# Latent attention: three heads' probabilities divided on ScalarE, turned in squares on VectorE and placed by transfers

## The chip, the core and the metric

The kernel runs on one core of a Trainium2 chip. The core has a matrix engine, TensorE (PE in the profile; PEld is its weight load), a vector engine (VectorE, DVE), a scalar engine (ScalarE, ACT), a general engine (GpSimd, POOL) and a sync engine (SyncE, SP) that here only issues transfers (DMAs). Each engine works through its own instructions in the order in which they were written; semaphores make one wait for another. Operands lie in SBUF (128 partitions), matrix products land in PSUM, of which this kernel uses seven banks in turn for products, and everything else is in the chip's main memory. The metric is the device time of one launch in microseconds (us).

## What is computed

Two layers (DEPTH = 2) over 256 tokens of width 1024, all in float32. The first layer's token mixer is latent attention with 8 heads, the second's is forgetting attention with 8 heads. Around each mixer stand two SwiGLU feed-forward blocks, and behind each layer a gated embedding is added. The change is in latent attention, whose core is this:

```python
def causal_block_attention(scores_fn, v, chunk_causal):
    for q0 in range(0, seq, Q_BLOCK):           # two blocks of 128 queries
        q1 = q0 + Q_BLOCK                       # block reads keys [0, q1)
        s = scores_fn(q0, q1)
        s = jnp.where(allowed, s, NEG_INF)
        probs = jax.nn.softmax(s, axis=-1).astype(v.dtype)
        outs.append(jnp.einsum('bhqk,bkhd->bqhd', probs, v[:, :q1]))

def mla_mixer(u, cos, sin, w_down, q_norm, w_uq, kv_norm, w_ukv, w_o):
    ...
    def scores(q0, q1):
        sc = (jnp.einsum('bqhd,bkhd->bhqk', q_nope[:, q0:q1], k_nope[:, :q1])
              + jnp.einsum('bqhr,bkr->bhqk', q_rope[:, q0:q1], k_rope[:, :q1]))
        return sc.astype(jnp.float32) * scale
    o = causal_block_attention(scores, v, chunk_causal=True)
    return o.reshape(b, s, MLA_HEADS * MLA_V) @ w_o
```

A head has three 128 x 128 blocks of probabilities: queries 0 to 127 against keys 0 to 127, and queries 128 to 255 against both key halves. The kernel holds them side by side, queries on the partitions, as one 128 x 384 tile. To multiply them with the values, TensorE needs keys on the partitions, so each head's 128 x 384 tile has to be turned.

## The kernel before

**Products.** Large products are computed as high times high, high times low and low times high, where a float32 operand is split into a rounded high half and the remainder as its low half. ScalarE writes the high half (L97 for weights, L559 for the heads' outputs), VectorE the low half (L101, L228). Weights come in pieces of 128 x 1024 through four raw buffers and seven pairs of high and low; a new fetch is issued on SP when VectorE has made a low half and so freed a raw buffer.

**Attention.** The function `attention` serves both mixers; `lag` is 3 for latent attention (called `late` in the code) and 2 for forgetting attention. It runs one loop of `H + lag` steps, and step h works on several heads at once. In latent attention step h does, in this order: `shares(h-2)`, the division of the probabilities by their sums (VectorE, L520 to L522); `low`, the low half of the output of the head whose values came last (VectorE, L228); `project(h)`, some remaining projections of queries and values; `turn(h-3)`, three transposes on TensorE (L543) and their evacuation by ScalarE into the tile ptS (L545); `scores(h-1)` (TensorE L782 and L784; maximum on VectorE L501, negated and scaled L505; exponentials with their sums on ScalarE L513 and L514); some units of the output projection (`fill_some`, L247 and L248); and `values(h-3)`, two products each for the two key halves (TensorE L557 and L558) with the evacuation of the high half by ScalarE (L559).

**Fills.** The output projection needs all heads, but a unit (one 128-column block of the output, one head) can run as soon as that head's high and low halves are there. A table `MLA_FILLS` gives the number of units for each step, and `ready` is the number of heads whose output the units may read. Up to four output blocks are open at once, each holding one PSUM bank. They fill TensorE while it would otherwise have too little to do.

**Forgetting attention.** Its first six heads (`moved=H - 2`) are already turned in another way: VectorE transposes the 32 x 32 squares inside the 128 x 384 tile (L526), four transfers put the squares in their places in main memory (L531) and one transfer reads the tile back (L536). The values product then reads the tile in the squares' order.

**Order of work.** There is no scheduler: the order on each engine is the order in which the code writes the instructions. Buffers rotate: 4 of the tile pr (probabilities), 3 of ptS (turned probabilities), 2 in main memory.

Of the kernel before, what the change touches and what calls it, by code (L numbers as in the profile page):

```python
# [11 lines left out]
F32 = mybir.dt.float32  # L12
# [7 lines left out]
P = 128  # L20
# [5 lines left out]
H = 8  # L26
# [114 lines left out]
def trunk(ctx, tc, xT, xt, pT, pos, freq, bf, lead0, lead1, ffn_in, ffn_out, w_down, w_uq, w_ukv, mla_o,  # L141
# [85 lines left out]
    def rest(hi, lo, src):  # L227
        nc.vector.tensor_sub(lo, src, hi.bitcast(F32))  # L228
# [255 lines left out]
            pass  # L484


    def attention(project, score, v, mask, scale, nxt, lag, fills, early, cumq=None, moved=0, room=None):
        late = lag > 2
        os = act.tile([P, H, 2, T], F32R, name="os", tag="u")
        probs = {}  # L490
        turned = {}
        lows = []

        def scores(h):
            ps = bank("psc", (P, 3 * P))
            score(h, (ps[:, :P], ps[:, P:]))
            m = work.tile([P, 2], F32, name="m", bufs=3)
            pr = work.tile([P, 3 * P], F32, name="pr", bufs=4)

            for i, a in enumerate((slice(0, P), slice(P, 3 * P))):  # L500
                nc.vector.tensor_tensor_reduce(pr[:, a], ps[:, a], mask(h)[i], 1.0, NEG, op0=ALU.add,  # L501
                                               op1=ALU.max, accum_out=m[:, i:i + 1])
            nm = work.tile([P, 2], F32, name="nm", bufs=3)
            if cumq is None:
                nc.vector.scalar_tensor_tensor(nm, m, -1.0, scale, op0=ALU.mult, op1=ALU.mult)  # L505
# [7 lines left out]
            nc.scalar.activation(pr[:, :P], pr[:, :P], AF.Exp, bias=nm[:, 0:1], scale=by[0], accum_out=den[:, 0:1])  # L513
            nc.scalar.activation(pr[:, P:], pr[:, P:], AF.Exp, bias=nm[:, 1:2], scale=by[1], accum_out=den[:, 1:2])  # L514
            probs[h] = pr, den

        def shares(h):
            pr, den = probs[h]
            inv = work.tile([P, 2], F32, name="inv", bufs=3)
            nc.vector.reciprocal(inv, den)  # L520
            nc.vector.tensor_scalar(pr[:, :P], pr[:, :P], inv[:, 0:1], None, op0=ALU.mult)
            nc.vector.tensor_scalar(pr[:, P:], pr[:, P:], inv[:, 1:2], None, op0=ALU.mult)  # L522
            if h < moved:
                pr, _ = probs.pop(h)
                squares = room[h % 2]
                nc.vector.transpose(squares.rearrange("p (k u c) -> p k u c", k=4, u=3),  # L526
                                    pr.rearrange("p (u k c) -> p k u c", u=3, k=4))
                turned[h] = dram.tile([P, 3 * P], F32, name="keys", bufs=2)
                to = turned[h].rearrange("(k r) (q n) -> q r k n", k=4, q=4)
                for q in range(4):  # L530
                    nc.sync.dma_start(to[q], squares[q * 32:(q + 1) * 32, :].rearrange("r (k n) -> r k n", k=4))  # L531

        def back(h):

            p = work.tile([P, 3 * P], F32, name="ptS", bufs=3)
            nc.sync.dma_start(p, turned[h])  # L536
            turned[h] = p

        def turn(h):
            pr, _ = probs.pop(h)  # L540
            pt = bank("pt", (P, 3 * P))
            for i in range(3):
                nc.tensor.transpose(pt[:, i * P:(i + 1) * P], pr[:, i * P:(i + 1) * P], ident)  # L543
            turned[h] = work.tile([P, 3 * P], F32, name="ptS", bufs=3)
            nc.scalar.activation(turned[h], pt, AF.Copy)  # L545

        def values(h):
            p = turned.pop(h)
            po = bank("po", (P, T))
            if h < moved:  # L550
# [6 lines left out]
            nc.tensor.matmul(to[0], v[:, 0, h * P:(h + 1) * P], p[0], start=True, stop=False)  # L557
            nc.tensor.matmul(to[1], v[:, 1, h * P:(h + 1) * P], p[1], start=False, stop=True)  # L558
            nc.scalar.activation(os[:, h, 0, :], po, AF.Copy)  # L559
            lows.append((os[:, h, 0, :], os[:, h, 1, :], po))  # L560

        def low():

            while lows:
                rest(*lows.pop())


        ws, pss, upto = {}, {}, {}
        ready = 0

        def fill(d, n):
            if d not in ws:
                ws[d], = W.get()

                pss[d] = bank("ps2", (P, 2, T) if d < KD - 3 else (P, T))
            if upto.setdefault(d, 0) < n:
                part(pss[d], ws[d], os, range(upto[d], n), H - 1)
                upto[d] = n

        def fill_some(n):  # L580
            while n > 0:
                d = min(ws, key=lambda d: (upto[d], d), default=None)
                if d is None or upto[d] >= ready:
                    if len(ws) == early:
                        return
                    d = len(ws)
                    upto[d] = 0
                m = min(ready - upto[d], n)
                if m <= 0:
                    return  # L590
                fill(d, upto[d] + m)
                n -= m

        def finish(d):
            W.done(ws[d])
            src = hT[:, d, :]
            for p in parts(pss[d]):
                nc.vector.tensor_add(src, p, src)
# [12 lines left out]

        for h in range(H + lag):
            if 0 <= h - 2 < H:
                shares(h - 2)
            low()
            if h == H and not late:
                W.pump()
            if late:

                ready = h - lag - 1  # L620
            if h < H:
                project(h, 0)
            fill_some(fills.get((h, 0), 0))
            if 0 <= h - lag < moved:
# [37 lines left out]
    def mla(norm, nxt):  # L662
# [26 lines left out]

        kq, v, kr = keys_values()  # L690
        kT, qT, qr = kq[:, :8, :], kq[:, 8:16, :], kq[:, 16:24, :]
        held = []
        halves = slice(0, ROPE), slice(ROPE, P)

# [89 lines left out]
                nc.tensor.matmul(dst[t], qr[:, h, t * P:(t + 1) * P], kr[:, h % 2, :(t + 1) * P], start=False,  # L784
                                 stop=t == 1)

        attention(project, score, v, lambda h: (chunks[:, P:], chunks), qscale, nxt, 3, MLA_FILLS, 4)


    def fox(norm, nxt):  # L790
# [98 lines left out]
        attention(project, score, v, lambda h: (early[:, h, :], drops[:, h, :]), FOX_SCALE, nxt, 2, FOX_FILLS, 4, cumq=cumq, moved=H - 2, room=squares)  # L889


    class Embedding:
# [429 lines left out]
```

## Time and profile before

| | before |
|---|---|
| median of 3 runs | 986.46 us (985.97 to 987.25) |
| profiled execution, its own time | 986.36 us |
| its span, first to last instruction | 984.5 us |
| TensorE busy | 975.1 us, 99% of the span |
| VectorE, ScalarE, GpSimd busy | 75%, 52%, 44% |
| granted TensorE clock, mean | 0.999 |
| latent attention's loop over heads | about 214 to 246 us of the span |
| VectorE busy from 215 to 240 us | 21.21 of 25 us |
| ScalarE busy from 215 to 240 us | 18.38 of 25 us |

The profile comes from one execution, and all positions are microseconds from the start of its span. In a timeline row stand the start, the duration, the engine, the line of the code, the operation, the tile written and the tile read, the shape and how many instructions were merged; in square brackets the time that the engine sat idle before and what ended it. Neighbouring instructions of one engine overlap, so what an instruction costs its engine is the distance of two starts rather than its duration.

### The profile page before, as it was taken

The numbers are of one execution on the slowest core, as the hardware profiler recorded it, in microseconds if no ns is written. First come the engines' busy times: TensorE is split into PE (matmuls) and PEld (weight loads), VectorE is DVE, ScalarE is ACT, GpSimd is POOL, SyncE is SP. The second block draws the span as 40 slices with busy tenths as digits, with TensorE's granted clock in tenths as the row PEclk, the third lists the DMA queues.
The fourth block names the chain that finished last, engine by engine and source line by source line (L and its number), as shares of the span: only waits on it lengthen the run. The fifth ranks groups of instructions, "written<-read, shape, count | busy, mean of one in ns | idle before, by whom it ended". The sixth has DMA issues, their size and how long they took to land.

```text
span 984.5 us, 15920 instructions
## 1 busy us (share of the span) xinstructions
PE 975.1 (99%) x5762; PEld 861.6 (88%) x5762; DVE 741.8 (75%) x1099; ACT 510.2 (52%) x798; POOL 438.1 (44%) x370
## 2 busy tenths in 40 slices
PE   9999999999999999999999999999999999999997
PEld 7888888998988888889888888889889888888886
DVE  6777878686887887666877886666897878876585
ACT  7555544466565454545555454546445555445361
POOL 0777731110377765111477773122231677772120
PEclk9999999999999999999999999999999999999999
DMA  8576666573376665665366666556773666666571
GB/s 317 184 252 209 204 181 188 182 208 117 125 218 213 194 187 177 190 205 172 107 195 211 196 185 196 178 174 224 235 224 112 214 210 204 193 176 198 142 256 54
DMA packets 67006, 187.26 MB, mean 190 GB/s; under 512 B 18628, under 2 KB 21072, under 8 KB 66800
## 3 DMA queue, kind: packets, MB, share of 16 engines
q1 hardware_dynamic: 65904, 183.94, 60.3%
q0 software_dynamic: 448, 1.45, 0.5%
q8 instruction: 46, 0.75, 0.3%
q10 hardware_dynamic: 576, 0.85, 0.3%
q14 instruction: 32, 0.26, 0.1%
HBM read 181.62 MB, written 2.24 MB: 187 GB/s over the span
## 4 chain that ended last, share of the span: by engine, by line
PE 94%; DVE 2%; ACT 1%; issue 1%; DMA 1%; POOL 0%; SPq 0%; POOLq 0%; DVEq 0%; ACTq 0%
PE po L247 17%; PE pu L247 16%; PE pg L247 16%; PE po L248 8%; PE pg L248 8%; PE pu L248 8%; PE ps L247 5%; PE ps L248 2%; PE ps L234 2%; PE ps L232 2%; PE ps L233 2%; PE pv L232 1%; PE pv L234 1%; PE po L557 1%; PE pv L233 1%
## 5 line engine op out<-in xcount | busy, mean ns | idle before, releaser
L101 DVE TENSOR_TENSOR wlo<-raw,whi 128x1024 fp32r<-128x1024 f32 (+2 forms) x339 | 415.0, 1230 | 27.9 <-ACT whi L97 27.1
L97 ACT ACTIVATE whi<-raw 128x1024 fp32r<-128x1024 f32 (+2 forms) x339 | 339.5, 1025 | 91.7 <-PE pg L247 35.5
L390 POOL TENSOR_TENSOR gu<-two 128x256 f32<-128x256 f32 x176 | 233.4, 1327 | 115.4 <-DVE two L388 107.8
L247 PE MATMUL pg<-u,whi 128*128 128x512 f32 x702 | 251.4, 395 | 0.3 <-DVE u L292 0.2
L247 PE MATMUL pu<-u,whi 128*128 128x512 f32 x702 | 250.9, 395 | 0.0
L247 PE MATMUL po<-hs,whi 128*128 128x512 f32 x704 | 246.8, 394 | 0.0
L248 PE MATMUL pg<-u,wlo 128*128 128x256 f32 x702 | 197.1, 281 | 0.6 <-DVE wlo L101 0.5
L248 PE MATMUL po<-hs,wlo 128*128 128x256 f32 x704 | 197.2, 280 | 0.0
L248 PE MATMUL pu<-u,wlo 128*128 128x256 f32 x702 | 196.8, 280 | 0.0
L247 PEld LDWEIGHTS po<-hs,whi 128*128 128x128 f32 x704 | 132.1, 188 | 31.3
L247 PEld LDWEIGHTS pg<-u,whi 128*128 128x128 f32 x702 | 131.8, 188 | 31.7 <-ACT whi L1099 0.5
L247 PEld LDWEIGHTS pu<-u,whi 128*128 128x128 f32 x702 | 131.8, 188 | 31.0
L248 PEld LDWEIGHTS pg<-u,wlo 128*128 128x128 f32 x702 | 132.0, 188 | 1.6 <-DVE wlo L101 0.8
L248 PEld LDWEIGHTS po<-hs,wlo 128*128 128x128 f32 x704 | 132.3, 188 | 0.0
L248 PEld LDWEIGHTS pu<-u,wlo 128*128 128x128 f32 x702 | 132.0, 188 | 0.0
L303 POOL TENSOR_TENSOR acc<-acc,sq 128x256 f32<-128x256 f32 x42 | 45.7, 1089 | 174.5 <-ACT sq L298 153.0
L408 POOL TENSOR_TENSOR hid<-sg,gu 128x256 f32<-128x256 f32 x88 | 112.7, 1281 | 6.9
L228 DVE TENSOR_TENSOR hs<-hid,hs 128x256 fp32r<-128x256 f32 x88 | 59.7, 679 | 57.3 <-ACT hs L224 57.3
L224 ACT ACTIVATE hs<-hid 128x256 fp32r<-128x256 f32 x88 | 36.5, 414 | 115.1 <-POOL hid L408 114.8
L388 DVE TENSOR_TENSOR two<-pg,rb 128x512 f32<-128x512 f32 x88 | 60.3, 685 | 32.1 <-PE pg L248 31.7
L287 ACT ACTIVATE u<-state 128x256 fp32r<-128x256 f32 x47 | 24.0, 511 | 102.9 <-DVE state L467 82.6
L467 DVE SCALAR_TENSOR_TENSOR state<-po,state 128x256 f32<-128x256 f32 x64 | 27.2, 424 | 57.3 <-PE po L248 56.1
(258 smaller groups left out, 1160.1 us busy)
## 6 DMA issues: line engine op xcount, KB each, us to landing
raw<-in_ffn_in_dram SPq DMA_DIRECT2D x172, 512.0 KB, 4.2
raw<-in_ffn_out_dram SPq DMA_DIRECT2D x64, 512.0 KB, 3.7
raw<-in_ffn_out_dram SPq DMA_DIRECT2D x32, 384.0 KB, 3.5
raw<-in_fox_qk_dram SPq DMA_DIRECT2D x16, 512.0 KB, 4.7
raw<-in_mla_o_dram SPq DMA_DIRECT2D x8, 512.0 KB, 4.4
raw<-in_ple_gate_dram SPq DMA_DIRECT2D x8, 512.0 KB, 4.3
raw<-in_fox_o_dram SPq DMA_DIRECT2D x8, 512.0 KB, 4.3
raw<-in_ple_rows_dram SPq DMA_DIRECT2D x8, 512.0 KB, 4.3
```

The source lines that it names most:

```text
L97: self.nc.scalar.activation(self.pairs[i][0][:, c], self.raws[i][:, c], AF.Copy)
L101: self.nc.vector.tensor_sub(lo[:, c], self.raws[i][:, c], hi[:, c].bitcast(F32))
L224: nc.scalar.activation(hi, src, AF.Copy)
L228: nc.vector.tensor_sub(lo, src, hi.bitcast(F32))
L232: nc.tensor.matmul(ps, w[0], x[0], start=first, stop=False)
L233: nc.tensor.matmul(ps, w[1], x[0], start=False, stop=False)
L247: nc.tensor.matmul(ps, hi, x[:, k], start=k == 0, stop=False)
L248: nc.tensor.matmul(ps[:, 1, :], lo, x[:, k, 0, :], start=False, stop=k == last)
L303: nc.gpsimd.tensor_add(new, self.acc, sq)
L388: nc.vector.tensor_mul(two, ps, norm.rb2)
L390: nc.gpsimd.tensor_add(gu[c, i], two[:, 0, :], two[:, 1, :])
L408: nc.gpsimd.tensor_mul(hid[c], gu.pop((c, 0)), gu.pop((c, 1)))
```

## The change

In latent attention heads 2, 3 and 4 (`moved=range(2, 5)`) are no longer turned by TensorE. Their division is done by ScalarE with two scaled copies (L523 of the new code) in place of two VectorE instructions. VectorE then transposes the 32 x 32 squares of the tile (L531) into one of two rooms in the unused part of the tile of rotary keys, behind the `low` of the same step. One transfer on SP writes the squares to main memory as they are (L535), and one step later four transfers, two on SP and two on GpSimd's queue, read them back in their places (L547). The values of these heads come one step later than before (`values(h - lag - 1)`). A new function `made` counts the heads that the fills may read; `low` takes waiting heads in order, since in step 8 the values of heads 4 and 5 come together. In forgetting attention the code is rewritten to the same effect as before.

```diff
-    def attention(project, score, v, mask, scale, nxt, lag, fills, early, cumq=None, moved=0, room=None):
+    def attention(project, score, v, mask, scale, nxt, lag, fills, early, cumq=None, moved=(), room=None):
...
-            nc.vector.tensor_scalar(pr[:, :P], pr[:, :P], inv[:, 0:1], None, op0=ALU.mult)
-            nc.vector.tensor_scalar(pr[:, P:], pr[:, P:], inv[:, 1:2], None, op0=ALU.mult)
...
+            for i, a in enumerate((slice(0, P), slice(P, 3 * P))):
+                if late and h in moved:
+                    nc.scalar.activation(pr[:, a], pr[:, a], AF.Copy, scale=inv[:, i:i + 1])
+                else:
+                    nc.vector.tensor_scalar(pr[:, a], pr[:, a], inv[:, i:i + 1], None, op0=ALU.mult)
+
+        def out(h):
+
+            pr, _ = probs.pop(h)
+            squares = room[h % 2]
+            nc.vector.transpose(squares.rearrange("p (k u c) -> p k u c", k=4, u=3),
+                                pr.rearrange("p (u k c) -> p k u c", u=3, k=4))
+            turned[h] = dram.tile([P, 3 * P], F32, name="keys", bufs=2)
+            if late:
+                nc.sync.dma_start(turned[h], squares)
+                return
...
         def back(h):
 
             p = work.tile([P, 3 * P], F32, name="ptS", bufs=3)
-            nc.sync.dma_start(p, turned[h])
+            if late:
+                src = turned[h].rearrange("(q r) (k n) -> k r q n", q=4, k=4)
+                for k in range(4):
+                    (nc.gpsimd if k % 2 else nc.sync).dma_start(
+                        p[k * 32:(k + 1) * 32, :].rearrange("r (q n) -> r q n", q=4), src[k])
+            else:
+                nc.sync.dma_start(p, turned[h])
             turned[h] = p
...
+        def made(step, other=None):
+
+            n = 0
+            while n < H and n + lag + (n in moved) <= (other if other and n in moved else step):
+                n += 1
+            return n
...
             if 0 <= h - 2 < H:
                 shares(h - 2)
+            if not late and h - 2 in moved:
+                out(h - 2)
             low()
+            if late and h - 2 in moved:
+                out(h - 2)
+            if late and h - lag in moved:
+                back(h - lag)
...
-            if moved <= h - lag:
+            if 0 <= h - lag and h - lag not in moved:
                 turn(h - lag)
...
-            ready = h - lag - (late or 0 < h - lag <= moved)
+            ready = made(h - 1 - late, h - 1)
             fill_some(fills.get((h, 1), 0))
-            if 0 <= h - lag - 1 < moved:
+            if h - lag - 1 in moved:
                 values(h - lag - 1)
-            if moved <= h - lag:
+            if 0 <= h - lag and h - lag not in moved:
                 values(h - lag)
...
-        attention(project, score, v, lambda h: (chunks[:, P:], chunks), qscale, nxt, 3, MLA_FILLS, 4)
+        attention(project, score, v, lambda h: (chunks[:, P:], chunks), qscale, nxt, 3, MLA_FILLS, 4, moved=range(2, 5),
+                  room=squares)
```

**VectorE, step 4: from the reciprocal of head 2's sums to the maximum of head 3.** Before (pr is the tile of probabilities, psc the scores, os the heads' outputs, po the values product, m the maxima):

```order
L520 RECIPROCAL inv<-den 128x2
L521 TENSOR_SCALAR pr<-pr,inv 128x128
L522 TENSOR_SCALAR pr<-pr,inv 128x256
L228 TENSOR_TENSOR os<-po,os 128x256
L501 ISA pr,m<-psc,chunks 128x128
```

Now:

```order
L520 RECIPROCAL inv<-den 128x2
L228 TENSOR_TENSOR os<-po,os 128x256
L531 STREAM_TRANSPOSE kqv<-pr 128x384
L501 ISA pr,m<-psc,chunks 128x128
L501 ISA m 128x1
```

The two divisions have left for ScalarE, and the transpose, which reads their result, stands ahead of the next head's maximum. Steps 5 and 6 look alike, except that in step 6 no low half stands between.

**TensorE, steps 6 and 7.** Before: three units of the output projection (ps_2658 and ps_2663 are its first two blocks), values of head 3, turn of head 4, scores of head 6, and the next units:

```order
L247 MATMUL ps_2663<-os,whi 128x512
L248 MATMUL ps_2663<-os,wlo 128x256
L557 MATMUL po<-ptS,kqv 128x256
L558 MATMUL po<-ptS,kqv 128x128
L543 MATMUL pt<-ident,pr 128x128 x3
L782 MATMUL psc<-kqv 128x128
L782 MATMUL psc<-kqv 128x256
L784 MATMUL psc<-kqv 128x128
L784 MATMUL psc<-kqv 128x256
L247 MATMUL ps_2663<-os,whi 128x512
L248 MATMUL ps_2663<-os,wlo 128x256
L247 MATMUL ps_2663<-os,whi 128x512
```

Now the values in this place are those of head 2 (ps_2665 is the second block):

```order
L247 MATMUL ps_2665<-os,whi 128x512
L248 MATMUL ps_2665<-os,wlo 128x256
L571 MATMUL po<-ptS,kqv 128x256
L572 MATMUL po<-ptS,kqv 128x128
L810 MATMUL psc<-kqv 128x128
L810 MATMUL psc<-kqv 128x256
L812 MATMUL psc<-kqv 128x128
L812 MATMUL psc<-kqv 128x256
L247 MATMUL ps_2665<-os,whi 128x512
L248 MATMUL ps_2665<-os,wlo 128x256
L247 MATMUL ps_2665<-os,whi 128x512
```

The turn is gone, and so are those of heads 2 and 3 in the two steps ahead. The last unit shown is, in both kernels, the first that reads head 2's output. In step 5 no values are computed any more.

**SP's queue.** Before, behind the rotary queries (kqv<-yz) come the weights of the next feed-forward block:

```order
L720 DMA kqv<-yz 64x256
L721 DMA kqv<-yz 64x256
L720 DMA kqv<-yz 64x256
L721 DMA kqv<-yz 64x256
L88 DMA raw<-in_ffn_in_dram 128x1024 x44
```

Now:

```order
L749 DMA kqv<-yz 64x256
L535 DMA keys<-kqv 128x384 x2
L547 DMA ptS<-keys 32x4x96 x2
L535 DMA keys<-kqv 128x384
L547 DMA ptS<-keys 32x4x96 x2
L88 DMA raw<-in_ffn_in_dram 128x1024
L547 DMA ptS<-keys 32x4x96 x2
```

Head 2's two reads stand behind head 3's write, head 3's behind head 4's write, and head 4's behind a weight fetch. GpSimd's queue has the other six reads, two for each head, with nothing between them.

More of the change, by code (lines that the diff above doesn't have):

```diff
@@ L520, in shares @@
             nc.vector.reciprocal(inv, den)
-            nc.vector.tensor_scalar(pr[:, :P], pr[:, :P], inv[:, 0:1], None, op0=ALU.mult)
-            nc.vector.tensor_scalar(pr[:, P:], pr[:, P:], inv[:, 1:2], None, op0=ALU.mult)
[L523 to L531, printed above, removed]
+            for i, a in enumerate((slice(0, P), slice(P, 3 * P))):
[12 more added lines that the diff above has]
+                return
+            to = turned[h].rearrange("(k r) (q n) -> q r k n", k=4, q=4)
+            for q in range(4):
+                nc.sync.dma_start(to[q], squares[q * 32:(q + 1) * 32, :].rearrange("r (k n) -> r k n", k=4))
         def back(h):
             p = work.tile([P, 3 * P], F32, name="ptS", bufs=3)
-            nc.sync.dma_start(p, turned[h])
+            if late:
[5 more added lines that the diff above has]
+                nc.sync.dma_start(p, turned[h])
             turned[h] = p
@@ L549, in values @@
             po = bank("po", (P, T))
-            if h < moved:
+            if h in moved:
                 p = p.rearrange("p (q u c) -> p u q c", q=4, u=3)
@@ L564, in low @@
             while lows:
-                rest(*lows.pop())
+                rest(*lows.pop(0))
+        def made(step, other=None):
[3 more added lines that the diff above has]
+            return n
         ws, pss, upto = {}, {}, {}
@@ L618, in attention @@
             if late:
-                ready = h - lag - 1
+                ready = made(h - 2)
             if h < H:
@@ L623, in attention @@
             fill_some(fills.get((h, 0), 0))
-            if 0 <= h - lag < moved:
+            if not late and h - lag in moved:
                 back(h - lag)
-            if moved <= h - lag:
+            if 0 <= h - lag and h - lag not in moved:
                 turn(h - lag)
@@ L691, in mla @@
         kT, qT, qr = kq[:, :8, :], kq[:, 8:16, :], kq[:, 16:24, :]
+        squares = [kr[:, a:a + 2, :].rearrange("p s n -> p (s n)")[:, :3 * P] for a in (2, 4)]
         held = []
@@ L887, in score @@
                                  start=t == 0, stop=t == 1)
-        attention(project, score, v, lambda h: (early[:, h, :], drops[:, h, :]), FOX_SCALE, nxt, 2, FOX_FILLS, 4, cumq=cumq, moved=H - 2, room=squares)
+        attention(project, score, v, lambda h: (early[:, h, :], drops[:, h, :]), FOX_SCALE, nxt, 2, FOX_FILLS, 4, cumq=cumq, moved=range(H - 2), room=squares)
     class Embedding:
```

## The prediction

> **What bounds the kernel now.** First the page's totals and its chain of waits:
>
> ```profile
> PE 975.1 (99%) x5762; PEld 861.6 (88%) x5762; DVE 741.8 (75%) x1099; ACT 510.2 (52%) x798; POOL 438.1 (44%) x370
> PE 94%; DVE 2%; ACT 1%; issue 1%; DMA 1%; POOL 0%; SPq 0%; POOLq 0%; DVEq 0%; ACTq 0%
> ```
>
> TensorE (PE) is busy almost all of the span and holds 94% of the chain. So a change is worth the PE work that it takes out, less the time for which it makes PE stand still. Next the timeline of PE in latent attention (start, duration; operations overlap, so the pitch is the difference of two starts):
>
> ```profile
> 227.82 0.70 PE L557 MATMUL po<-ptS,kqv 128*128 128x256 f32 x2
> 228.57 0.49 PE L543 MATMUL pt<-ident,pr 128*128 128x128 f32 x3
> 228.90 0.82 PE L782 MATMUL psc<-kqv 128*128 128x128 f32 x4
> ...
> 231.26 0.59 PE L557 MATMUL po<-ptS,kqv 128*128 128x256 f32 x2
> 231.92 0.49 PE L543 MATMUL pt<-ident,pr 128*128 128x128 f32 x3
> ...
> 233.91 0.40 PE L247 MATMUL ps<-os,whi 128*128 128x512 f32 x1
> ...
> 234.97 0.59 PE L557 MATMUL po<-ptS,kqv 128*128 128x256 f32 x2
> ```
>
> These are steps 5 to 7 of the loop over heads: the values of head 2, the turn and the values of head 3 (231.26), the turn of head 4 and, past the scores of head 6, units of the output projection. The unit at 233.91 is the first that reads head 2. Now the softmax on VectorE (DVE) and ScalarE (ACT) in the same stretch:
>
> ```profile
> 230.28 0.17 DVE L520 RECIPROCAL inv<-den 128x2 f32<-128x2 f32 x1 [0.64 <-ACT pr L514]
> 230.95 0.42 DVE L228 TENSOR_TENSOR os<-po,os 128x256 fp32r<-128x256 f32 x1
> 231.28 0.28 DVE L501 CUSTOM_DVE_ANT_0 pr<-psc,chunks 128x128 f32<-128x128 f32 x1
> 233.41 0.17 DVE L520 RECIPROCAL inv<-den 128x2 f32<-128x2 f32 x1 [0.15 <-ACT pr L514]
> 232.21 0.49 ACT L513 ACTIVATE pr<-pr,nm,qscale 128x128 f32<-128x128 f32 x1 [0.37 <-DVE nm L505]
> 232.61 0.19 ACT L513 ACTIVATION_READ_ACCUMULATOR pr<-pr,nm,qscale 128x1 f32 x1
> ```
>
> There is a loop: reciprocal of one head, its division, the maximum of the next head, its exponentials on ACT, the next reciprocal. It takes 233.41 - 230.28 = 3.13 us a head: 1.00 from reciprocal to next maximum, 2.13 from there to the next reciprocal. Nothing on DVE waits for PE in it, while PE needs about as long for a head (231.92 - 228.57 = 3.35 from turn to turn). It is a second, nearly binding chain, hidden by slack: head 2's low half (230.95 + 0.42 = 231.37) is used at 233.91, 2.5 us later.
>
> **The change, part by part.** *Removed from PE:* three turns, each 228.90 - 228.57 = 0.33 us of pitch: -1.0 us. Three ACT evacuations of them and six DVE divisions go too, neither on PE.
>
> *Lengthened: the loop.* For heads 2, 3 and 4 the next maximum on DVE now stands behind a square transpose, which stands behind two ACT divisions. No row shows such a division, so it is bounded by ACT rows of the grouped view; the transpose is the one of forgetting attention:
>
> ```profile
> L1012 ACT ACTIVATE fin<-fin,r 128x384 f32<-128x384 f32 x1 | 0.6, 615 | 2.2 <-POOL r L1019 2.2
> L863 ACT ACTIVATE zt<-pv,wide 128x8 f32<-128x8 f32 x2 | 0.5, 260 | 0.0
> L513 ACT ACTIVATE pr<-pr,nm,qscale 128x128 f32<-128x128 f32 x8 | 3.9, 494 | 6.5 <-DVE nm L505 6.5
> L287 ACT ACTIVATE u<-state 128x256 fp32r<-128x256 f32 x47 | 24.0, 511 | 102.9 <-DVE state L467 82.6 <-DVE state L944 10.1 <-DVE state L598 10.0
> 700.39 0.58 DVE L526 STREAM_TRANSPOSE kqv<-pr 128x384 f32<-128x384 f32 x1
> 700.89 0.65 DVE L872 TENSOR_TENSOR two<-ps,rb 128x512 f32<-128x512 f32 x1
> ```
>
> Between 8 and 384 columns the scaled copy grows by (615 - 260) / 376 = 0.94 ns a column: 0.37 us for 128, 0.49 for 256. Overlapped like the exponential and its neighbour (232.61 - 232.21 = 0.40 for a 0.49 us instruction), the pair takes 0.77. As the upper bound stand 0.49 and 0.51 (the last two ACT groups), end to end with a 0.03 hand-over: 1.03. Reciprocal 0.17, two hand-overs of 0.03, the pair, 0.50 for the transpose (700.89 - 700.39): 1.50 to 1.76 where 1.00 stood. That is +0.5 to +0.76 a head, +1.5 to +2.3 for three. I take +1.9, near the middle: the second division waits for its own engine, the first for DVE. So head 5's reciprocal goes from 233.41 to 235.3.
>
> *Moved: values of 2, 3 and 4, one step later.* Head 2's values now come in step 6, so its low half stands behind head 5's reciprocal and divisions: 235.3 + 0.67 (the 230.95 - 230.28 above) + 0.42 = 236.4. The PE unit at 233.91 is still at the same place in step 7 and still reads head 2. It cannot start before 236.4: 2.5 us later. By then PE has done values of heads 0 to 2, where before it had done 0 to 3; that group is still to come, 231.92 - 231.26 = 0.66 us. The turns of 2, 3 and 4, on the other hand, lay ahead of this point before and are already inside it. From here the instructions are the same: **+2.5 + 0.66 = +3.15 us**, with the bounds of the divisions +2.75 to +3.55.
>
> *Added: transfers.* These decide when PE stands still, as long as they stay inside the wait above. The rows are the sync queue's (SP) timeline and the groups of issues, with median times to landing at the end:
>
> ```profile
> 225.35 0.59 SPq L721 DMA_DIRECT2D kqv<-yz  x1
> 701.00 1.78 SPq L531 DMA_DIRECT2D keys<-kqv  x4
> 705.10 0.34 SPq L536 DMA_DIRECT2D ptS<-keys  x1
> keys<-kqv SPq DMA_DIRECT2D x24, 48.0 KB, 2.9
> ptS<-keys SPq DMA_DIRECT2D x6, 192.0 KB, 3.0
> DMA to landing us min/median/max: 2.1/3.0/4.2
> rbs<-row POOLq DMA_DIRECT2D x1, 256.0 KB, 4.6
> 224.03 0.17 DVE L520 RECIPROCAL inv<-den 128x2 f32<-128x2 f32 x1 [0.50 <-ACT pr L514]
> ```
>
> Head 2: reciprocal 224.03, transpose done 1.7 later at 225.75, SP free of the rotary transfers at 225.94, so the write lands near 229.0. The two reads on SP stand behind head 3's write: its reciprocal is at 224.03 + 2.13 + 1.63 = 227.8, its transpose done at 229.5. After 0.34 for that write and 0.45 a read (1.78 / 4), the last read is issued at 230.3 and lands at 233.2 (232.4 to 234.5). GpSimd's (POOL) pair, issued at 229.0 and a little after, lands between 231.2 (with the 2.1) and 234.0 (with the 4.6 of its 256 KB row). PE would come to these values at 231.26 - 2 x 0.33 - 0.75 (head 2's group at its old place, 228.57 - 227.82) = 229.85. So PE stands 3.3 us there, then works 233.91 - 231.26 - 0.33 = 2.3 us up to the unit that reads head 2 and stands about 0.9 more. Both waits less the 1.0 removed give 3.2, the same sum. The transfer would decide only if it landed after 236.4 - 2.3 = 234.1. Head 3's values are due 1.06 (234.97 - 233.91) after that unit, at 237.5; its last read is issued about 233.9, behind head 4's write, and lands at 236.8, in the worst row 238.1. Head 4 is wanted 4.2 us later still.
>
> *What hides the rest.* POOL and the weight prefetch on SP:
>
> ```profile
> 250.60 0.74 POOL L303 TENSOR_TENSOR acc<-sq 128x256 f32<-128x256 f32 x1 [39.62 <-ACT sq L298]
> 233.28 26.43 SPq L88 DMA_DIRECT2D raw<-in_ffn_in_dram  x6
> 252.87 1.99 ACT L97 ACTIVATE whi<-raw 128x1024 fp32r<-128x1024 f32 x2
> ```
>
> POOL has nothing else to do. The first weight fetch slips from 233.28 to about 235.5, behind the lengthened loop, and is wanted at 252.87; later fetches stand behind head 4's reads on SP until about 237.5. Were that cover gone, each us over would cost one. In forgetting attention every engine keeps its order.
>
> **Sum.** The profiled execution took 986.36 us (span 984.5), 0.10 under the median of 986.46, so both give the same answer: 986.36 + 3.15 = **989.5 us**, its own range 988.6 to 990.6.
>
> **The rivals.** *Cover holds, not slower than before (12%).* One mechanism: the reads land by 229.85 and the low half is there when wanted, so that only the turns count. The slack of 2.5 us at 233.91 and the two steps of room speak for it; against it, the low half moves a whole step of 3.13 even if the division and the transpose cost nothing, and a write and a read of 2.1 us each end after 229.85. All cover kept: 986.36 - 1.0 = 985.4. With the loop unchanged but the step lost, the unit starts at 233.41 + 1.09 = 234.5, which is +0.6 + 0.66 = +1.25, or 987.6. From +0.7 (the 1.97 us bound less 1.25) of loop on, it is slower. Half of this rival lies on either of these two.
>
> *Late transfers (15%).* If POOL's reads take as long as its 256 KB one, or each SP leg its 4.2, a head arrives 1 to 2 us after 234.1, or head 3 after 237.5: 990.5 to 991.5. [...] Against: 192 KB a head is small, and the next weight fetch is issued at 233.28 only.
>
> *A slow clock after the wait (8%).* PE's first rows, the first window's granted clock (before the 0.63) and PE's longest wait later on:
>
> ```profile
> 1.08 3.60 PE L1090 MATMUL cold<-warm 128*128 128x256 bf16 x16 [1.08 <-DVE warm L1087]
> 5.12 0.41 PE L1110 MATMUL pu<-u,whi 128*128 128x256 f32 x1
> 6.11 0.28 PE L1110 MATMUL pu<-u,wlo 128*128 128x256 f32 x1
> 0.00:5.00 5.00, 3.92 (x19) 2.99 (x20) 1.46 (x5) 2.24 (x5) 1.03 (x9) 1.00 0.63 196
> PE pg L248 <- DVE wlo L101: 0.5, 1, 0.5
> ```
>
> After the idle start the same product takes 0.41 us and later 0.28; the granted clock says 1.00 in either case, so it shows only in durations. It lasts some 5 us (1.08 to 6.11). Afterwards PE never stands longer than 0.5. If a wait of 3.3 us brings that slow state back for 5 us, the 2.3 us of work behind the wait become 3.4 and fill the second wait, and the other 1.6 us lose a third (1 - 0.28 / 0.41), 0.5 us; if it holds twice as long, 2.1 us. That is 990.0 to 991.6, about 990.6. [...]
>
> **How the numbers follow.** Forecast 62%, cover 12%, late transfers 15%, slow clock 8%, something unseen 3%, split. This kernel's measurement tells about 0.2% (1.97 us) from no change. The forecast, late transfers and slow clock are slower; the cover case is the same on both its ends; faster would need more than all the PE work removed. So slower 0.85, same 0.13, faster 0.02. The range must reach into the cover case and to late transfers: 988.0 to 991.6.
>
> **What would show it.** Right: the turns x3 missing three times on PE; a PE wait of about 3 us ended by DMA before head 2's values and one of about 1 us ended by DVE in the projection; reciprocals 3.6 to 3.9 us apart for three heads. Wrong: no PE wait over 1 us between 225 and 240; matmuls of 0.41 after it; or a wait after 250, which I cost at nothing.

## The result, and the profile after

| | before | after |
|---|---|---|
| median | 986.30 us (985.67 to 987.25, 6 runs) | 990.20 us (989.62 to 990.50, 6 runs) |
| ratio, with its 95% interval | | 1.0039 (1.0028 to 1.0049) |
| profiled execution, its span | 986.36, 984.5 us | 990.30, 988.3 us |
| attention: first scores product to last unit of the projection (start to start) | 37.08 us | 40.60 us |

The change makes the kernel 3.9 us slower. In the traces 3.5 us of it lie inside latent attention; the rest is spread over the span, and repeated executions differ by as much (985.67 to 987.25 before, 989.62 to 990.50 after). Three of the six executions of the changed kernel show the mean granted clock of the profiled one, 0.996, and took 990.30 to 990.50 us; the other three show 0.998 or 0.999 and took 989.62 to 990.11. The first scores start at 214.27 us before and at 213.70 after, so positions after are about 0.6 us early against those that the prediction quotes.

First the page of the changed kernel: TensorE's busy time and the chain of waits.

```profile
PE 975.8 (99%) x5753; PEld 861.3 (87%) x5753; DVE 743.8 (75%) x1096; ACT 511.4 (52%) x801; POOL 442.5 (45%) x376
PE 89%; DVE 4%; DMA 2%; ACT 2%; SPq 1%; issue 1%; POOL 1%; POOLq 0%; ACTq 0%; DVEq 0%
```

The three turns are gone, nine products fewer, yet PE is busy 0.7 us longer, and its share of the chain falls from 94% to 89%. The list of PE's waits says on whom it now waits (total, times, longest):

```profile
PE po L571 <- DMA ptS<-keys: 2.2, 1, 2.2
...
PE po L571 <- ACT ptS L559: 0.5, 1, 0.5
```

The first is new; the second, for a turned tile, was there before too, at another head and with 0.2 us. There is no wait for DVE in the projection, which was the second one forecast. The timeline of PE around them (start, duration, then what was waited for in brackets):

```profile
224.90 0.70 PE L571 MATMUL po<-ptS,kqv 128*128 128x256 f32 x2 [0.51 <-ACT ptS L559]
...
229.90 0.28 PE L248 MATMUL ps<-os,wlo 128*128 128x256 f32 x1
232.33 0.67 PE L571 MATMUL po<-ptS,kqv 128*128 128x256 f32 x2 [2.15 <-DMA ptS<-keys]
...
233.06 1.31 PE L810 MATMUL psc<-kqv 128*128 128x128 f32 x4
234.16 1.49 PE L812 MATMUL psc<-kqv 128*128 128x128 f32 x4
235.09 0.99 PE L247 MATMUL ps<-os,whi 128*128 128x512 f32 x1
235.88 0.41 PE L248 MATMUL ps<-os,wlo 128*128 128x256 f32 x1
236.09 0.63 PE L247 MATMUL ps<-os,whi 128*128 128x512 f32 x1
```

The unit at 236.09 is the first that reads head 2; the next one starts at 236.71. Behind the wait, scores that took 0.82 us a group take 1.31 and 1.49, and a unit's first product takes 0.99. The table by stretches says why; the column behind the engines' busy times is the granted clock:

```profile
232.00:233.00 1.00, 0.67 (x4) 0.65 (x5) 0.96 (x7) 0.59 (x1) 0.31 (x1) 1.00 0.18 52
233.00:234.00 1.00, 1.00 (x7) 0.91 (x6) 1.00 (x1) 0.98 (x3) 0.00 (x0) 0.63 0.79 257
...
235.00:236.00 1.00, 1.00 (x4) 0.80 (x3) 0.62 (x4) 0.40 (x1) 1.00 (x2) 0.50 0.91 160
...
236.50:237.00 0.50, 0.50 (x4) 0.43 (x3) 0.50 (x2) 0.44 (x2) 0.00 (x0) 0.84 1.00 382
```

The clock is halved from about 233.25 (0.75 us of the second stretch at 0.50 give its 0.63) to about 236.66 (0.16 us of the last stretch at 0.50 give its 0.84): 3.4 us. Last, the softmax loop on DVE, whose reciprocals show its pace, and head 2's low half:

```profile
223.47 0.17 DVE L520 RECIPROCAL inv<-den 128x2 f32<-128x2 f32 x1 [0.50 <-ACT pr L514]
224.50 0.58 DVE L531 STREAM_TRANSPOSE kqv<-pr 128x384 f32<-128x384 f32 x1 [0.34 <-ACT pr L523]
225.00 0.25 DVE L501 CUSTOM_DVE_ANT_0 pr<-psc,chunks 128x128 f32<-128x128 f32 x1
...
234.22 0.17 DVE L520 RECIPROCAL inv<-den 128x2 f32<-128x2 f32 x1
...
234.89 0.42 DVE L228 TENSOR_TENSOR os<-po,os 128x256 fp32r<-128x256 f32 x1
```

From reciprocal to next maximum it takes 1.53 us (225.00 - 223.47) where 1.00 stood, and three heads take 10.75 (234.22 - 223.47) where 9.38 stood (233.41 - 224.03): 3.58 a head in place of 3.13. Head 2's low half ends at 235.31. So in this execution the unit at 236.09 did not wait for it: PE came to the unit 0.78 us later still, because the transfer had held it until 232.33 and the slow clock then stretched the work in between.

So the sum in the trace runs as follows, on PE's starts counted from the first scores. The unit that reads head 2 starts 22.39 us in (236.09 - 213.70), before 19.64 (233.91 - 214.27): **+2.75**. From there to the last unit it takes 18.21 and before 17.44: **+0.77**, of which 0.66 are head 3's values.

### The profile page after: what moved, and what is told of

The parts are those of the page before. It is cut to its first block, busy times and chain, and to the rows that moved or that the text cites. A ratio compares the mean times of both kernels' runs of the same rounds, so it can differ in the third digit from the quotient of the medians.

```text
span 988.3 us, 15924 instructions
## 1 busy us (share of the span) xinstructions
PE 975.8 (99%) x5753; PEld 861.3 (87%) x5753; DVE 743.8 (75%) x1096; ACT 511.4 (52%) x801; POOL 442.5 (45%) x376
## 4 chain that ended last, share of the span: by engine, by line
PE 89%; DVE 4%; DMA 2%; ACT 2%; SPq 1%; issue 1%; POOL 1%; POOLq 0%; ACTq 0%; DVEq 0%
PE pu L247 16%; PE pg L247 16%; PE po L247 15%; PE pg L248 8%; PE pu L248 8%; PE po L248 7%; PE ps L247 5%; PE ps L248 2%; DVE wlo L101 2%; PE ps L232 1%; PE ps L234 1%; PE ps L233 1%; SPq L944 1%; PE pv L232 1%; PE pv L234 1%
## 5 line engine op out<-in xcount | busy, mean ns | idle before, releaser
L402 ACT ACTIVATE sg<-gu 128x256 f32<-128x256 f32 x88 | 36.8, 418 | 64.8 <-POOL gu L390 64.8
```

Of the source, the lines that this page charges most:

```text
L402: nc.scalar.activation(sg, gu.pop((c, 0)), AF.Silu)
```

## The experiments

The theory tested first is the prediction's: the loop is lengthened and head 2's low half has lost a step, so this low half sets the unit that reads head 2, and the transfers are hidden behind it; to this the profile after adds that the slow clock costs about 1 us more. The rivals put the loss down to the transfers alone, to ScalarE's divisions, or to the loop by itself. The ratios are to the kernel before, on the same chip.

**1. Keep the matrix engine busy in the wait.** Sixteen small products that nobody reads stand ahead of head 2's values.

```diff
+            if late and h - lag - 1 == moved[0]:
+                spare = psm.tile([P, T], F32, name="spare", tag="small")
+                for _ in range(16):
+                    nc.tensor.matmul(spare, warm[:, :P], warm, start=True, stop=True)
             if h - lag - 1 in moved:
                 values(h - lag - 1)
```

> The changed kernel with 16 small bf16 products (128 x 256, result unused) on TensorE just ahead of head 2's values, where the changed kernel's trace has TensorE stand still for 2.15 us; they take about 16 x 0.11 = 1.8 us, so they fit into the wait. Theory 1 (the halved granted clock that the changed kernel's trace shows from 233.3 to 236.7 us follows from the wait and costs time): the granted clock stays 1.00 through 230 to 240 us, the scores behind the wait go back from 2.03 to 1.13 us, and a wait of about 0.6 us for VectorE's low half of head 2 appears at the first projection unit that reads it; net about 1.1 us less than the changed kernel, so 989.1 us. Rival (those products are slow for another reason, such as the transfers that run beside them, or the slow stretch is covered by the wait for the low half anyway): 990.0 to 990.4 us.

Measured: 989.45 us (988.97 to 990.02, 8 runs), ratio 1.0029 (1.0018 to 1.0040). Its timeline of PE:

```profile
230.17 1.92 PE L670 MATMUL spare<-warm 128*128 128x256 bf16 x16
232.86 0.67 PE L571 MATMUL po<-ptS,kqv 128*128 128x256 f32 x2 [0.77 <-DMA ptS<-keys]
...
233.58 0.82 PE L814 MATMUL psc<-kqv 128*128 128x128 f32 x4
...
235.51 0.50 PE L247 MATMUL ps<-os,whi 128*128 128x512 f32 x1
235.51 0.19 PEld L247 LDWEIGHTS ps<-os,whi 128*128 128x128 f32 x1 [0.42 <-DVE os L228]
```

The granted clock is 1.00 from 222 to 245 us, and the scores take their 0.82 again. The unit that reads head 2 starts 0.73 us earlier than in the changed kernel (21.66 us after the first scores at 213.85, against 22.39), right behind the low half (here 235.04 + 0.42 = 235.46), for which its weight load stood 0.42 us. Attention takes 39.83 us in this trace, 0.77 less than with the slow stretch; that is the price of the slow clock in one execution. The medians differ by about as much, 0.75, but they alone would not tell it, since only a part of the changed kernel's executions show the lower mean clock. What is left is a wait for DVE, as forecast, though shorter than the 0.6 expected here.

**2. The divisions back on VectorE.** Transposes, transfers and the later step stay.

```diff
-                if late and h in moved:
+                if False:
                     nc.scalar.activation(pr[:, a], pr[:, a], AF.Copy, scale=inv[:, i:i + 1])
```

> The changed kernel with the divisions of heads 2, 3 and 4 back on VectorE; squares, transfers and the later values stay. Theory 1: on VectorE reciprocal 0.20, two divisions 0.47, low half 0.33 and transpose 0.50 make the same 1.5 us from reciprocal to next maximum as the ScalarE route (1.53 us measured), so head 2's transfer lands at the same time; the 0.5 us wait for head 1's turned tile, whose evacuation the ScalarE divisions delay, goes, but the wait behind it grows by the same: 990.2 us, within 0.3. Rival (the hand-over to ScalarE and back is what costs): three hand-overs and the 0.5 us wait gone, 988.5 to 989.5 us.

Measured: 990.55 us (989.80 to 991.28, 4 runs), ratio 1.0040 (1.0025 to 1.0055). The engine that divides does not matter here (990.20 with ScalarE's divisions). DVE's timeline tells what does:

```profile
223.61 0.17 DVE L520 RECIPROCAL inv<-den 128x2 f32<-128x2 f32 x1 [0.51 <-ACT pr L514]
...
224.61 0.57 DVE L531 STREAM_TRANSPOSE kqv<-pr 128x384 f32<-128x384 f32 x1
225.10 0.25 DVE L501 CUSTOM_DVE_ANT_0 pr<-psc,chunks 128x128 f32<-128x128 f32 x1
227.21 0.17 DVE L520 RECIPROCAL inv<-den 128x2 f32<-128x2 f32 x1 [0.64 <-ACT pr L514]
```

The loop is as long as with ScalarE's divisions (227.21 - 223.61 = 3.60 us). What it got longer by is the transpose: 225.10 - 224.61 = 0.49. And PE's wait:

```profile
232.64 1.19 PE L571 MATMUL po<-ptS,kqv 128*128 128x256 f32 x2 [3.09 <-DMA ptS<-keys]
```

Head 1's values no longer wait for ScalarE here, and PE only stands longer at the next place: 3.09 instead of 2.15. That wait in the changed kernel lies inside the following one and costs nothing of its own.

**3. No transfers.** The values product reads the squares where VectorE has put them. The placing of the blocks is left out, so the output of heads 2 to 4 is another one.

```diff
             if late:
-                nc.sync.dma_start(turned[h], squares)
+                turned[h] = squares
                 return
...
         def back(h):
+            if late:
+                return
```

> The changed kernel without the trip through main memory: the values of heads 2, 3 and 4 read the squares where VectorE left them, so these heads' output is another one (the blocks of keys are not put in their places); all else stays. Theory 1 (head 2's low half, one step later and behind the lengthened softmax loop, sets the end, and transfers only decide where TensorE stands still): no wait ended by a transfer, TensorE comes to the first unit that reads head 2 at about 232.3 us and waits there for VectorE until about 235.3, 3 us; 989.4 us if the clock stays up, up to 991 if it is halved after that wait. Rival (the transfers are what costs): the waits go, 985.5 to 987 us.

Measured: 989.56 us (988.17 to 991.55, 10 runs), ratio 1.0033 (1.0023 to 1.0042). PE's timeline:

```profile
232.31 0.70 PE L573 MATMUL po<-kqv 128*128 128x256 f32 x2 [2.12 <-DVE kqv L531]
...
235.37 0.51 PE L247 MATMUL ps<-os,whi 128*128 128x512 f32 x1 [0.47 <-DVE os L228]
```

The first wait was not meant: head 4's transpose uses the room of head 2's squares and stands ahead of head 2's values in the program. It keeps PE standing as long as the transfers did, 2.12 us against 2.15, so this run does not show a PE that never stands there. But the wait does not decide. PE comes to the unit that reads head 2 and still waits there for DVE's low half, and starts at 235.37, against 235.51 in experiment 1 with all its transfers. So **without any transfer the time is the same as with them** (989.56, and 989.45 with transfers and a full clock; attention takes 39.71 and 39.83 us in the two traces). The low half is set by the loop and by the step in which it stands: it is written behind head 5's reciprocal, at 234.23 in this trace, and from head 4's reciprocal (230.65) to there DVE waits for ScalarE alone and never for PE. Without the first wait PE would only have stood longer at this unit.

**4. Two heads, further apart.** Heads 4 and 6 are moved in place of 2, 3 and 4.

```diff
-        ... MLA_FILLS, 4, moved=range(2, 5),
+        ... MLA_FILLS, 4, moved=(4, 6),
```

> The changed kernel with heads 4 and 6 moved in place of 2, 3 and 4: no head's reads stand behind another head's write on the sync queue, and their values fall in steps 8 and 10, where TensorE has projection units to do. Theory 1 (the loss comes from where the heads lie, not from the way they are turned): two turns less on TensorE, -0.66 us, no wait for a transfer over 0.3 us, up to 0.4 us lost at the tail where the values of heads 6 and 7 stand together: 985.6 to 986.1 us. Rival (the route itself costs, a step of lag and the lengthened loop wherever it is used): 987 to 988.5 us.

Measured: 988.61 us (988.19 to 990.13, 10 runs), ratio 1.0021 (1.0012 to 1.0030). The expectation failed. Here PE waits for the reads:

```profile
239.98 0.67 PE L571 MATMUL po<-ptS,kqv 128*128 128x256 f32 x2 [1.05 <-DMA ptS<-keys]
...
246.04 0.67 PE L571 MATMUL po<-ptS,kqv 128*128 128x256 f32 x2 [0.70 <-DMA ptS<-keys]
```

The chain of waits around the first of them, and the groups of issues with the median time to landing:

```profile
234.27 0.60 POOL ptS L547
234.87 4.91 DMA ptS<-keys
```

```profile
ptS<-keys POOLq DMA_DIRECT2D x4, 48.0 KB, 4.3
ptS<-keys SPq DMA_DIRECT2D x4, 48.0 KB, 4.1
```

In the changed kernel the same reads land after 2.0 (SP) and 2.1 us (POOL). Here weight fetches of 512 KB were issued on SP at 233.75 and 236.73, beside them. The changed kernel has both cases in one trace: the reads of heads 2 and 3 land after 1.9 to 2.2 us, those of head 4, issued from 234.61 on behind a weight fetch (234.16), after 3.8 to 4.1. So the late landings go with the fetches beside them, though no run takes the fetches away. The kernel loses 2.3 us although two turns, 0.67, are saved.

**5. No transfers and no later step.** As in 3, and the values come in their old step; `made`, which counts the heads that the fills may read, follows. The loop stays long.

```diff
-            while n < H and n + lag + (n in moved) <= (other if other and n in moved else step):
+            while n < H and n + lag + (n in moved and not late) <= (other if other and n in moved and not late else step):
...
-            if late and h - lag in moved:
-                back(h - lag)
...
-            if h - lag - 1 in moved:
+            if not late and h - lag - 1 in moved:
                 values(h - lag - 1)
-            if 0 <= h - lag and h - lag not in moved:
+            if 0 <= h - lag and (late or h - lag not in moved):
                 values(h - lag)
```

> The three heads are still divided by ScalarE and transposed in squares by VectorE, but there are no transfers (the values product reads the squares where they stand, so the output of heads 2 to 4 is another one) and their values come in their old step. So the lengthened loop stays, and the lost step and the route go. Theory (the lost step, which puts head 2's low half behind head 5's reciprocal, makes the loop count; the loop by itself is hidden): head 2's low half stands behind head 4's reciprocal (230.64 in the changed kernel) and is done at about 231.7, before the unit that reads it. No wait of TensorE over 0.6 us; the three turns are saved, 1.0, against 0.5 to 0.7 for head 1's values waiting for ScalarE's evacuation: 985.6 to 986.4. Rival (the loop of 3.58 us a head bounds TensorE by itself, whatever the step): 987.3 to 988.5, with waits of scores or values on VectorE.

Measured: 985.76 us (984.89 to 986.17, 10 runs), ratio 0.9993 (0.9984 to 1.0002). Attention is 36.66 us long, 0.42 less than before. PE's list of waits and the low half of head 2 on DVE:

```profile
PE po L571 <- ACT ptS L559: 0.7, 2, 0.5
```

```profile
230.31 0.17 DVE L520 RECIPROCAL inv<-den 128x2 f32<-128x2 f32 x1 [0.58 <-ACT pr L514]
230.58 0.42 DVE L228 TENSOR_TENSOR os<-po,os 128x256 fp32r<-128x256 f32 x1
...
233.90 0.17 DVE L520 RECIPROCAL inv<-den 128x2 f32<-128x2 f32 x1
```

The reciprocals are as far apart as in the changed kernel (233.90 - 230.31 = 3.59), but the low half of head 2 ends at 231.00, and PE waits nowhere for it. **The long loop alone does not make the kernel slower; it costs through the lost step**, which puts the low half behind a reciprocal that comes 3.59 us later. No run has the lost step with the short loop, so how the cost divides between the two is not shown. The experiment also bounds what the idea could bring for these three heads: with the placing for nothing, the time cannot be told from before. Three turns are 1.0 us, and of that head 1's values, which wait for ScalarE behind the new divisions, take back half.

**6. Other work in the wait.** Only the table of fills is another one: eight units in step 6, none in step 7 and the first place of step 8.

```diff
-MLA_FILLS = {(6, 1): 3, (7, 1): 4, (8, 0): 1, (8, 1): 5, (9, 0): 4, (9, 1): 3, (10, 0): 2, (10, 1): 2}
+MLA_FILLS = {(6, 1): 8, (8, 1): 6, (9, 0): 3, (9, 1): 3, (10, 0): 2, (10, 1): 2}
```

> Only the table of fills is another one: eight units of the projection in step 6 (all that heads 0 and 1 allow) in place of three, none in step 7 and in the first place of step 8, six in the second place of step 8. So TensorE has work of its own (five units of 0.35, 1.75 us) where it stood 2.15 us, and the first unit that reads head 2 stands behind head 5's turn and head 7's scores. Theory (the loss is idle time of TensorE and the slow clock that follows it, both of which other work can fill): wait for head 2 about 0.4, granted clock 1.00 throughout, head 3's values wait up to 1.0 for their reads (issued 232.8 to 233.6), none for head 2's low half: 986.3 to 987.3. Rival (the loop and the transfers only push the wait on, to head 3's values, the turn of head 5 or the banks of PSUM): a wait of 1.5 us or more behind it and 988 to 990.

Measured: 988.54 us (987.82 to 989.45, 10 runs), ratio 1.0020 (1.0010 to 1.0029). The granted clock stays at 1.00 from 228 to 244 us, and 1.7 us of the loss are back, though not the 2.9 or more that were expected. PE's timeline:

```profile
224.80 0.70 PE L571 MATMUL po<-ptS,kqv 128*128 128x256 f32 x2 [0.51 <-ACT ptS L559]
...
231.33 0.40 PE L247 MATMUL ps<-os,whi 128*128 128x512 f32 x1
...
232.41 0.67 PE L571 MATMUL po<-ptS,kqv 128*128 128x256 f32 x2 [0.57 <-DMA ptS<-keys]
...
233.79 0.82 PE L812 MATMUL psc<-kqv 128*128 128x128 f32 x4
...
235.16 0.67 PE L571 MATMUL po<-ptS,kqv 128*128 128x256 f32 x2 [0.55 <-DMA ptS<-keys]
...
237.34 0.58 PE L247 MATMUL ps<-os,whi 128*128 128x512 f32 x1
...
238.33 0.50 PE L247 MATMUL ps<-os,whi 128*128 128x512 f32 x1 [0.29 <-DVE os L228]
```

The long wait has become several short ones: head 2's and head 3's reads, then the low half of head 3. Each costs more than its idle time. By pitch, the first is 232.41 - 231.33 = 1.08 where a unit takes 0.35, so 0.73 for a wait of 0.57; the same way the second costs 0.72, the third 0.45, and head 1's, no longer inside another, 0.67. Together 2.57, less the turns 1.0: +1.57, and attention is 1.63 longer than before.

**7. Another route for head 4's write.** As 6, and that write goes to GpSimd's queue behind its reads of head 3, so that SP's reads of head 3 stand behind no write.

```diff
-                nc.sync.dma_start(turned[h], squares)
+                (nc.gpsimd if h == moved[-1] else nc.sync).dma_start(turned[h], squares)
```

> As the kernel with the other fills, and head 4's write goes to GpSimd's queue, behind that queue's reads of head 3, so that SP's two reads of head 3 stand behind no write. Theory (head 3's reads are late only since they stand on SP behind head 4's write, which waits for its transpose): they are issued when head 3's write has landed, about 231.3 instead of 232.8, land by 233.5 to 234, and the wait before head 3's values goes: 0.5 to 1.0 less than the kernel with the other fills alone, 985.8 to 986.6. Rival (the landing itself, not the queue, is what is late): the same time as that kernel within 0.3.

Measured: 987.94 us (987.41 to 988.50, 10 runs), ratio 1.0017 (1.0008 to 1.0026). The median is 0.6 us under experiment 6, but the intervals overlap, and in the profiled executions attention is as long (38.72 and 38.71). The wait for head 3's reads has gone, as expected; in its place the low half of head 3 is waited for longer:

```profile
PE ps L247 <- DVE os L228: 0.6, 1, 0.6
```

The wait before head 2's values is 0.40 instead of 0.57; the profile puts it down to head 4's transpose, and why they should wait for that is not shown. Whether the route gains a few tenths stays open; it does not beat the kernel before. No version that computes the whole result did.

## Why the prediction was right, and where it was not

The time (989.5 against 990.2), its range and the sign were right, and experiments 1, 3 and 5 confirm the mechanism as long as the clock stays up: the low half of head 2, a step later behind a longer loop, sets the first unit that reads head 2. In the profiled execution of the changed kernel the slow clock came last instead, by 0.78 us. So the sum is composed differently, and one of the prediction's own signs of being wrong appeared, products of 0.41 us after the wait (at 235.88). Of its signs of being right the missing turns and the wait for a transfer came; the wait for DVE did not, and the reciprocals, 3.58 us apart, just missed 3.6.

- *Turns removed, -1.0.* Right: three groups fewer, and 0.42 of it shows in experiment 5.
- *Loop, +1.5 to +2.3 for three heads, taken +1.9.* The step "I take +1.9, near the middle" was mis-sized: 10.75 - 9.38 = +1.37, just under the lower bound. One head's 1.53 lies at the lower end of 1.50 to 1.76: the pair of divisions took 0.80 us as one overlapped group, and the reason given for the middle, a wait of the first division for DVE, cost next to nothing. Experiment 2 says what the term should have been: the transpose alone, 0.49.
- *The unit that reads head 2, +2.5.* Measured +2.75, for another reason. With the loop as measured the unit would have come at about 235.4, as in experiments 1 and 3, which is 21.7 us after the first scores: +2.0. The slow clock added 0.7.
- *Head 3's values behind it, +0.66.* Right: +0.77, the unit at 236.09 being slow by another 0.27 (0.62 to the next in place of 0.35).
- *First wait, 3.3 us.* It was 2.15. The last read landed at 232.24 (chain, below), by the common start 0.4 us ahead of the 233.2 forecast, and PE came 0.9 later, mostly (0.67 by pitch, as in experiment 6) since head 1's values waited for ScalarE, whose evacuation is queued behind the new divisions. The prediction did not name that wait, although it had to ask what stands behind the divisions on ScalarE; experiment 2 shows that it was absorbed.
- *Second wait, 0.9 us for DVE.* It did not come, as the slow clock filled it; with a full clock it is there (0.47 in experiment 3, 0.42 on the weight load in experiment 1).
- *"Late transfers", 15%.* Not for heads 2 and 3 in this kernel. Experiment 4 shows that it was the right fear for other places: with weight fetches beside them the reads took 4.1 to 4.3 us (median), one of them 4.9. Experiment 6 adds that, with the long wait filled, PE still stands for the reads of heads 2 and 3, 0.57 and 0.55 us.
- *"A slow clock after the wait", 8%.* This happened. The forecast cost of that rival, about 1.1 over the forecast, was near what experiment 1 took off (0.75). The 8% was the author's estimate: the trace before has no wait over 0.5 us after the start that could have shown it. Here the clock was halved after 2.15 us of waiting, less than the 3.3 forecast, and for 3.41 us where the prediction took 5 (last section). The prediction also took the 1.00 at the start to mean that a slow state shows in durations only; here the granted clock shows it, at 0.50.
- *"Cover holds", 12%.* Fell: neither the room of two steps nor the slack of 2.5 us covered a whole lost step.

So an over-sized term (0.5) and one left to a rival (0.7 and 0.1) cancelled in part: attention came out 0.4 us longer than forecast, and the other 0.3 of the 0.7 us lie outside it. That the number came so near is in part luck; the median also lies in the band of the slow-clock rival (990.0 to 991.6), which had been given 8%.

## What to carry to other kernels

Work that is moved off a bound engine must keep its step: a helper that is hidden while it has slack can become the bound as soon as its last consumer moves behind one more turn of its loop, however cheap the new instructions are. Price a stall by when the engine gets going again at full speed, not by its idle time, and try first whether work of its own can be put there. Before a route through main memory is built, leave it out in an experiment: if the time with a free route is no better than before, the route need not be built.

## What the hardware showed unexpectedly

**A wait of about 2 us was followed by a halved clock in one trace and not in another.** In the changed kernel, with a wait of 2.15 us, the granted clock went to 0.50 about 0.9 us after PE had resumed, and stayed there for 3.41 us, from 233.25 to 236.66. In experiment 2, with a wait of 3.09 us, it was at 0.50 from 232.33 to 235.74, also 3.41 us; it had fallen 0.3 us before PE resumed (232.64), and PE's first products were already slow (1.19 us in place of 0.67). In experiment 3 a wait of 2.12 us at the same place left the clock at 1.00. In the rows that follow the first number behind a stretch's length is PE's busy time, and the third from the end is the granted clock. The changed kernel:

```profile
229.84:233.25 3.41, 1.26 (x8) 0.92 (x8) 1.93 (x9) 2.75 (x8) 1.97 (x4) 1.00 0.44 120
233.25:236.66 3.41, 3.41 (x12) 2.86 (x12) 2.87 (x11) 2.25 (x7) 1.09 (x2) 0.50 0.70 192
```

Experiment 2:

```profile
228.92:232.33 3.41, 0.63 (x4) 0.31 (x2) 2.67 (x13) 2.12 (x5) 2.16 (x4) 1.00 0.43 118
232.33:235.74 3.41, 3.10 (x10) 2.77 (x11) 2.73 (x10) 2.50 (x6) 0.79 (x3) 0.50 0.63 144
```

Experiment 3:

```profile
222.00:230.00 8.00, 7.49 (x44) 6.31 (x42) 5.89 (x22) 5.34 (x18) 0.00 (x0) 1.00 0.46 154
230.00:235.00 5.00, 2.78 (x16) 2.11 (x14) 3.39 (x13) 4.33 (x12) 0.00 (x0) 1.00 0.00 0
235.00:240.00 5.00, 4.63 (x28) 4.20 (x29) 3.84 (x15) 3.41 (x8) 0.00 (x0) 1.00 0.65 197
```

In the 3.41 us ahead of the fall PE was busy for 1.26 us in the changed kernel and for 0.63 us in experiment 2. In experiment 3 it was busy for about as little as in the changed kernel in the 3.41 us that end with its wait (3.41 - 2.12 = 1.29), and the clock did not fall. So neither the length of the wait nor PE's work just ahead tells these two traces apart, and what does is not shown. The mean clock differs between executions of one kernel too: it was 0.996 in three of the six executions of the changed kernel and in four of the ten of experiment 3, and 0.997 to 0.999 in the others; where it fell in the executions without a profile is not on record.

**The 48 KB reads took twice as long to land where 512 KB fetches ran beside them.** They landed after 2.0 to 2.1 us (median) in the changed kernel, where all transfers together moved 52 to 114 GB/s from 230 to 233 us, and after 4.1 to 4.3 us in experiment 4, beside 512 KB fetches (253 GB/s from 235 to 240 us); within the changed kernel it was 1.9 to 2.2 us for heads 2 and 3 and 3.8 to 4.1 for head 4. The way of head 2 through main memory, in the changed kernel's chain:

```profile
225.49 3.80 DMA keys<-kqv
...
229.57 0.60 POOL ptS L547
230.17 2.07 DMA ptS<-keys
```

It is 6.8 us from the write's issue to the first product (232.33 - 225.49), two heads' worth of the loop, for 192 KB.
